# Two transformer blocks in split float32: one weight load for both halves of the activations

## The chip, the cores and the metric

The kernel runs on one core of a Trainium2 chip. The metric is the device time of one launch in microseconds; the time before is the median of three runs. One launch computes both blocks once, for 256 tokens.

## The reference

`reference` sends `x` (256 tokens, 1024 features) through `first_block` and then `second_block`. The first block has two layers, each a mixer and an MLP with a residual around both, and a norm at the end:

```python
for i in range(DEPTH):                 # 2 layers
    hn = rms_norm(x, norm_mix[i])
    mix = even_mixer(...) if i % 2 == 0 else odd_mixer(...)
    x = x + mix
    x = x + sqrelu_mlp(rms_norm(x, norm_mlp[i]), mlp_w1[i], mlp_w2[i])
return rms_norm(x, norm_final)
```

`even_mixer` is a sparse attention beside a differential attention, `odd_mixer` a block attention, each between an input projection and an output projection. `sqrelu_mlp` is `square(relu(hn @ w1)) @ w2` with 4096 hidden features. The second block has one input projection for a convolution with a gated linear recurrence (`xa`, `ga`, 1280 features each), a forgetting attention (`q`, `k`, `v`) and two gates. The branches go through `w_proj_a` and `w_proj_b`, are merged by the gates, and go through `w_out` and a norm; a feed-forward part follows (up to 2 x 3072, convolution, gelu, product, down) with a last norm.

## The kernel before

Activations lie with the features on partitions: `x` is 8 tiles of 128 features by 256 tokens. Nearly all work is products with weights that are read once, as 1 MB chunks (pool `rawp`, 3 buffers, SyncE's queue). A chunk is cut into units of 8 k-tiles by 128 columns, and each unit is split into a high part `whi` (a ScalarE cast, L220) and a low part `wlo` (a VectorE subtraction, L221), both float32r; `w_next` keeps some units ahead. Activations are split in the same way (`split`, L253 to L257): `gh`, `gl` for the normed input of a projection, `hh`, `hl` for the hidden features, `oh`, `ol` for attention outputs, `yh`, `yl` for the recurrence's output. One k-step of a product is three matmuls of 128x128 weights by 256 tokens (`mm3`, L261): high by high, high by low, low by high.

Sums are kept in the PSUM pool `psg`, three buffers of one bank, `[128, 2, 256]`. The order on every engine is that in which the code issues, since the order is fixed by hand: a stage is a generator (`gen_pair`, `gen_nat`, `gen_deep`, `gen_half`), `weave` alternates it with the attention steps, and short work is put off by `later`, `tick` and `pend.step`. `gen_pair` (L384) works on pairs of 128-column tiles, both in one bank, and calls `evac` after the pair. Where a stage begins before its norm is known, it starts on two pairs at once (`kouter`, orders K422, K2, K1). `gen_nat` puts the tokens on the output's partitions, for values. `gen_deep` (L446) is for long sums, one tile per bank (MLP-down, projection a, FFN-down), and `gen_half` (L470) for output projections in two halves of k: the first half is woven with attention and adds to `x`, the second adds, splits and squares for the next norm.

In an MLP, `evac` (L1158) is a VectorE operation that scales by the norm `rb` and clips (L1159), a square (L1160), a cast to `hh` (L253, ScalarE) and the low part `hl` (L254, VectorE). MLP-down adds each tile to `x` (L708) and splits it for the next projection. Output projections add pairs (L718, L726). The norm's factor comes from sums of squares over the features (L317, L324), a diagonal `dg` (L355) and a broadcast product (L360), copied to `rb` (L364). In block 2 projection a multiplies by its gate (L1538), projection b does so and adds (L1550, L1553), and then splits for the projection by `w_out` (o2).

## Time and profile before

| | |
|---|---|
| time, median of three runs | 1174.48 us (1172.11 to 1174.5) |
| span of the profiled execution | 1170.4 us |
| TensorE busy, matmuls | 1138.5 us, 97% |
| TensorE busy, weight loads (beside matmuls) | 1088.1 us, 93% |
| VectorE busy | 793.4 us, 68% |
| ScalarE busy | 625.7 us, 53% |
| GpSimd busy | 190.3 us, 16% |
| DMA | 171 GB/s over the span |

The profiled execution is one of the program; its span runs from the first instruction to the last, and the run's time holds some 4 us more. Matmuls are pipelined, so the duration of one (some 280 ns) says little of its cost; the distance from one start to the next does. A wait is put down to what came last. Stages of the span: layer 0 mixer up to about 155 us, its MLP to 338, layer 1 mixer to 453, its MLP to 638, the recurrence with gates and values to 745, forgetting attention with projections a and b to 910, o2 and its norm to 950, FFN-up to 1065, FFN-down and the last norm to the end.

### The profile page before, as it was taken

How to read it: one execution, taken by the hardware profiler on the slowest of the kernel's cores; microseconds unless marked ns; L12 is line 12 of the kernel's file. 1: busy time of each engine (PE TensorE's matmuls, PEld its weight loads, DVE VectorE, ACT ScalarE, POOL GpSimd, SP SyncE). 2: the span in 40 equal slices, each digit the busy share in tenths (PEclk: the TensorE clock that was granted, in tenths of full speed). 3: DMA queues.
4: the chain of work that ended last, by engine and by line, in shares of the span. 5: the costliest groups of instructions: out<-in, count | busy, mean ns of one | idle time of the engine just before them, and what ended most of it. 6: DMA issues, size and time to landing. Idle time of an engine off the chain costs nothing.

```text
span 1170.4 us, 22694 instructions
## 1 busy us (share of the span) xinstructions
PE 1138.5 (97%) x9343; PEld 1088.1 (93%) x9343; DVE 793.4 (68%) x1404; ACT 625.7 (53%) x1112; POOL 190.3 (16%) x228
## 2 busy tenths in 40 slices
PE   8999999999999999999999999999999999999996
PEld 7987799999999889999999897999999999999996
DVE  5767766674545777566445787766567689999842
ACT  4346555653444545565434577644454556676641
POOL 2014320000010123000001000042310123222211
PEclk9999999999999999999999999999999989999998
DMA  8832244555444334355455453564555525445641
GB/s 331 290 136 73 74 180 145 212 202 199 177 184 180 141 113 145 144 214 206 158 215 198 153 204 109 175 239 141 166 180 197 173 99 167 164 175 180 212 149 36
DMA packets 31303, 200.01 MB, mean 171 GB/s; under 512 B 3594, under 2 KB 6042, under 8 KB 9056
## 3 DMA queue, kind: packets, MB, share of 16 engines
q1 hardware_dynamic: 28832, 187.23, 44.6%
q0 software_dynamic: 2080, 11.08, 2.9%
q8 instruction: 73, 1.20, 0.4%
q14 instruction: 30, 0.25, 0.1%
q10 hardware_dynamic: 288, 0.26, 0.1%
HBM read 197.43 MB, written 3.22 MB: 171 GB/s over the span
## 4 chain that ended last, share of the span: by engine, by line
PE 78%; DVE 14%; ACT 3%; issue 2%; POOL 2%; DMA 1%; SPq 0%; POOLq 0%; ACTq 0%
PE g L262 22%; PE g L264 21%; PE g L263 21%; DVE y L1643 4%; DVE wlo L221 4%; PE rgp L1414 2%; PE g L435 2%; PE g L436 2%; PE g L437 2%; PE pt L623 1%; PE o L673 1%; DVE u L1631 1%; ACT whi L220 1%; PE s L579 1%; DVE y L1655 1%
## 5 line engine op out<-in xcount | busy, mean ns | idle before, releaser
L221 DVE TENSOR_TENSOR wlo<-raw,whi 128x1024 fp32r<-128x1024 f32 (+2 forms) x356 | 420.3, 1212 | 114.2 <-ACT whi L220 113.9
L262 PE MATMUL g<-gh,whi 128*128 128x256 f32 x1632 | 463.7, 284 | 3.2 <-ACT whi L220 1.7
L264 PE MATMUL g<-gh,wlo 128*128 128x256 f32 x1632 | 460.1, 282 | 3.1 <-DVE wlo L221 3.1
L263 PE MATMUL g<-gl,whi 128*128 128x256 f32 x1632 | 457.6, 280 | 0.5 <-DVE gl L257 0.4
L220 ACT CAST whi<-raw 128x1024 fp32r<-128x1024 f32 (+2 forms) x356 | 349.9, 1024 | 18.0 <-PE g L263 8.4
L262 PEld LDWEIGHTS g<-gh,whi 128*128 128x128 f32 x1632 | 309.1, 189 | 10.6 <-issue 5.4
L264 PEld LDWEIGHTS g<-gh,wlo 128*128 128x128 f32 x1632 | 309.2, 189 | 7.2 <-DVE wlo L221 7.1
L263 PEld LDWEIGHTS g<-gl,whi 128*128 128x128 f32 x1632 | 309.4, 190 | 1.1 <-DVE gl L257 0.7
L262 PE MATMUL g<-hh,whi 128*128 128x256 f32 x704 | 199.4, 283 | 1.3 <-DVE u L1631 1.3
L264 PE MATMUL g<-hh,wlo 128*128 128x256 f32 x704 | 199.3, 283 | 0.2 <-DVE wlo L221 0.2
L263 PE MATMUL g<-hl,whi 128*128 128x256 f32 x704 | 199.2, 283 | 0.0
L262 PEld LDWEIGHTS g<-hh,whi 128*128 128x128 f32 x704 | 135.1, 192 | 1.5 <-ACT q L1652 1.5
L264 PEld LDWEIGHTS g<-hh,wlo 128*128 128x128 f32 x704 | 135.1, 192 | 0.4 <-DVE wlo L221 0.4
L263 PEld LDWEIGHTS g<-hl,whi 128*128 128x128 f32 x704 | 135.1, 192 | 0.0
L317 POOL TENSOR_TENSOR acc<-acc,sq 128x256 f32<-128x256 f32 x53 | 42.4, 806 | 465.2 <-ACT sq L313 464.3
L612 POOL TENSOR_TENSOR p<-p,rr 128x384 f32<-128x384 f32 x56 | 50.1, 895 | 205.9 <-DVE rr L607 92.8
L597 ACT ACTIVATE p<-p,nm 128x256 f32<-128x256 f32 x112 | 49.9, 448 | 56.0 <-DVE nm L588 55.8
L1643 DVE SCALAR_TENSOR_TENSOR y<-u,cw,y 128x255 f32<-128x255 f32 (+1 forms) x96 | 60.1, 685 | 0.0
L262 PE MATMUL g<-oh,whi 128*128 128x256 f32 x192 | 55.6, 290 | 0.0
L264 PE MATMUL g<-oh,wlo 128*128 128x256 f32 x192 | 54.3, 283 | 0.0
L263 PE MATMUL g<-ol,whi 128*128 128x256 f32 x192 | 54.2, 282 | 0.0
L1160 ACT ACTIVATE u<-u 128x512 f32<-128x512 f32 x32 | 20.2, 632 | 61.9 <-DVE u L1159 61.9
(317 smaller groups left out, 1455.8 us busy)
## 6 DMA issues: line engine op xcount, KB each, us to landing
raw<-in_w_in_dram SPq DMA_DIRECT2D x30, 1024.0 KB, 4.9
raw<-in_w_up_dram SPq DMA_DIRECT2D x24, 1024.0 KB, 4.9
raw<-in_w_m1a_dram SPq DMA_DIRECT2D x16, 1024.0 KB, 4.8
raw<-in_w_m2a_dram SPq DMA_DIRECT2D x16, 1024.0 KB, 5.0
raw<-in_w_m1b_dram SPq DMA_DIRECT2D x16, 1024.0 KB, 4.9
raw<-in_w_m2b_dram SPq DMA_DIRECT2D x16, 1024.0 KB, 4.9
raw<-in_w_od_dram SPq DMA_DIRECT2D x12, 1024.0 KB, 4.8
raw<-in_w_dn_dram SPq DMA_DIRECT2D x12, 1024.0 KB, 4.8
```

Of the source, the lines that this page charges most:

```text
L220: nc.scalar.copy(out=hi[:, a:b], in_=t[:, off + a:off + b])
L221: nc.vector.tensor_tensor(out=lo[:, a:b], in0=t[:, off + a:off + b], in1=hi[:, a:b].bitcast(F32), op=ALU.subtract)
L262: nc.tensor.matmul(out=o, lhsT=wh, rhs=xh, start=start, stop=False, skip_group_check=skip)
L263: nc.tensor.matmul(out=o, lhsT=wh, rhs=xl, start=False, stop=False, skip_group_check=skip)
L264: nc.tensor.matmul(out=o, lhsT=wl, rhs=xh, start=False, stop=stop, skip_group_check=skip)
L317: nc.gpsimd.tensor_tensor(out=self.acc, in0=self.acc, in1=dst, op=ALU.add)
L435: nc.tensor.matmul(out=ps[:, b, :], lhsT=xh[:, k, bs], rhs=wh[:, k % 4, :], start=(k == 0), stop=False)
L436: nc.tensor.matmul(out=ps[:, b, :], lhsT=xh[:, k, bs], rhs=wl[:, k % 4, :], start=False, stop=False)
L437: nc.tensor.matmul(out=ps[:, b, :], lhsT=xl[:, k, bs], rhs=wh[:, k % 4, :], start=False, stop=(k == KT - 1))
L597: nc.scalar.activation(out=p[:, c0:c1], in_=p[:, c0:c1], func=AF.Exp, scale=-1.0, bias=nm[:, b:b + 1], accum_out=sm[:, b:b + 1],)
L612: nc.gpsimd.tensor_tensor(out=pv, in0=pv, in1=w, op=ALU.mult)
L1643: nc.vector.scalar_tensor_tensor(out=y[:, a, d:], in0=u[:, a, 0:T - d], scalar=cw[:, w, c:c + 1], in1=y[:, a, d:], op0=ALU.mult, op1=ALU.add)
```

## The change

High and low parts of an activation lie side by side in one tile (`Halves`), so that a k-step is two matmuls (`mm2`): the high weights by both parts, 512 columns, into the two halves of a bank, and the low weights by the high part, 256 columns, into the first half. A bank then holds one 128-column tile instead of a pair. The two sums are added afterwards: in `gen_pair` ScalarE copies the second half to the target in SBUF and VectorE adds the first half (`add`, put off by one step); in `take` (projections a and b, FFN-down) the same in one place; for residuals VectorE adds each half to `x` (`add_both`). The values of layer 1 and block 2 use 512-column weights as the moving side (`gen_wide`). The start on two pairs at once, the small gate products, layer 0's values and the last up-projection (block 2's FFN) keep three matmuls. The number of matmul rows of the program goes from 8676 to 6422 on TensorE. Layout changes on the host follow (`_wides`), and some comments are removed. The diff, cut:

```diff
+class Halves:
+
+    def __init__(self, t):
+        self.t = t
+        self.h = t[:, :, 0, :]
+        self.l = t[:, :, 1, :]
+
+    def both(self, k):
+        return self.t[:, k].rearrange("p a t -> p (a t)")
...
-    gh = xp.tile([128, KT, T], FR, name="gh")
-    gl = xp.tile([128, KT, T], FR, name="gl")
+    gg_ = xp.tile([128, KT, 2, T], FR, name="gg_")
+    g_ = Halves(gg_)
+    gh, gl = g_.h, g_.l
...
+    def mm2(ps, wh, wl, X, k, start, stop):
+
+        nc.tensor.matmul(out=ps.rearrange("p a t -> p (a t)"), lhsT=wh, rhs=X.both(k), start=start, stop=False, skip_group_check=True)
+        nc.tensor.matmul(out=ps[:, 0, :], lhsT=wl, rhs=X.h[:, k, :], start=False, stop=stop, skip_group_check=True)
+
+    def take(dst, ps):
+        nc.scalar.copy(out=dst, in_=ps[:, 1, :])
+        nc.vector.tensor_tensor(out=dst, in0=ps[:, 0, :], in1=dst, op=ALU.add)
...
+        wide = getattr(evac, "dst", None)
+        for j in range(j0, npair if wide else 0):
+            D_ = Ctl()
+            for a in range(2):
+                ps = psg.tile([128, 2, T], F32, tag="g", name="g")
+                wh, wl, (nk, ncol) = w_next()
+                if last and j == npair - 1 and a == 1:
+                    w_ahead(4)
+                for k in range(nk):
+                    mm2(ps, wh[:, k, :], wl[:, k, :], X, k, k == 0, k == nk - 1)
+                    if k == 3:
+                        pend.step()
+                        yield
+                if a == 0:
+                    D_.d = wide(first + j)
+                d = D_.d[:, a, :]
+                nc.scalar.copy(out=d, in_=ps[:, 1, :])
+
+                def add(j=j, a=a, d=d, ps=ps, D_=D_):
+                    nc.vector.tensor_tensor(out=d, in0=ps[:, 0, :], in1=d, op=ALU.add)
+                    if a == 1:
+                        pend.ready(lambda: evac(first + j, D_.d))
+
+                later(1, add)
+                pend.step()
+                yield
+        for j in range(npair if wide else j0, npair):
             ps = psg.tile([128, 2, T], F32, tag="g", name="g")
             for a in range(2):
...
-                        mm3(pss_[j][:, 0, :], wh[:, k, :], wl[:, k, :], xh[:, kk, :], xl[:, kk, :], kk == 0, kk == nu * nk - 1)
+                        mm2(pss_[j], wh[:, k, :], wl[:, k, :], X, kk, kk == 0, kk == nu * nk - 1)
...
-                        evac(j, pss_[j][:, 0, :])
+                        evac(j, pss_[j])
...
-            ps = psg.tile([128, 2, T], F32, tag="g", name="g")
             for a in range(2):
+                ps = psg.tile([128, 2, T], F32, tag="g", name="g")
                 for k in range(nk):
-                    mm3(ps[:, a, :], wh[:, k, a * 128:a * 128 + 128], wl[:, k, a * 128:a * 128 + 128],
-                        xh[:, k0 + k, :], xl[:, k0 + k, :], k == 0, k == nk - 1)
-                if a == 0:
-                    tick()
-                    yield
-            evac(j, ps)
-            tick()
-            yield
+                    mm2(ps, wh[:, k, a * 128:a * 128 + 128], wl[:, k, a * 128:a * 128 + 128], X, k0 + k, k == 0, k == nk - 1)
+                evac.wide(j, a, ps)
+                tick()
+                yield
 
...
-            nc.vector.tensor_tensor(out=x[:, j, :], in0=x[:, j, :], in1=ps, op=ALU.add)
+            add_both(j, ps)
...
+    def add_both(i, ps):
+        for s in range(2):
+            nc.vector.tensor_tensor(out=x[:, i, :], in0=x[:, i, :], in1=ps[:, s, :], op=ALU.add)
...
+        def wide(j, a, ps):
+            i = 2 * j + a
+            add_both(i, ps)
+            split(gh[:, i, :], gl[:, i, :], x[:, i, :], V(gain, i))
+            later(2, lambda: norm.add(x[:, i, :]))
+
+        f.wide = wide
...
-        hh = hp.tile([128, 32, T], FR, name="hh")
-        hl = hp.tile([128, 32, T], FR, name="hl")
+        H = Halves(hp.tile([128, 32, 2, T], FR, name="hh"))
+        hh, hl = H.h, H.l
 
         def evac(j, ps):
-            u = hp.tile([128, 2, T], F32, tag="u", name="u", bufs=2)
+            u = ps if j > 1 else evac.dst(j)
...
+        evac.dst = lambda j: hp.tile([128, 2, T], F32, tag="u", name="u", bufs=3)
         pend = Pend(norm)
-        run(gen_pair(16, gh, gl, evac, pend, kouter=K422))
-        run(gen_deep(8, 4, hh, hl, residual_evac(nrm, gain_next, nrm2)))
+        run(gen_pair(16, g_, evac, pend, kouter=K422))
+        run(gen_deep(8, 4, H, residual_evac(nrm, gain_next, nrm2)))
         st.close()
...
-    run(gen_nat(4, gh, gl, evac_v1, pend))
-    run(gen_pair(1, gh, gl, evac_qk("q"), pend))
-    run(gen_pair(1, gh, gl, evac_qk("k"), pend))
+    run(gen_wide(2, gh, gl, evac_v1, pend))
+    run(gen_pair(1, g_, evac_qk("q"), pend))
+    run(gen_pair(1, g_, evac_qk("k"), pend))
...
+        def wide(j, a, ps):
+            i = 2 * j + a
+            t = fp.tile([128, T], F32, tag="pat", name="pbt", bufs=2)
+            take(t, ps)
+            nc.vector.scalar_tensor_tensor(out=t, in0=tb[:, i, :], scalar=1.0, in1=t, op0=ALU.add, op1=ALU.mult)
+            nc.vector.tensor_tensor(out=ta[:, i, :], in0=ta[:, i, :], in1=t, op=ALU.add)
+            if last:
+                split(gh[:, i, :], gl[:, i, :], ta[:, i, :])
...
+    def gen_wide(n, xh, xl, evac, pend):
+
+        for j in range(n):
+            pss_ = [psg.tile([128, 2, T], F32, tag="g", name="g") for _ in range(2)]
+            for u in range(4):
+                wh, wl, (nk, ncol) = w_next()
+                for b in range(2):
+                    bs = slice(b * 128, b * 128 + 128)
+                    o = pss_[b].rearrange("p a t -> p (a t)")
+                    for k in range(2):
+                        kk = 2 * u + k
+                        nc.tensor.matmul(out=o, lhsT=xh[:, kk, bs], rhs=wh[:, k, :], start=(kk == 0), stop=False)
+                        nc.tensor.matmul(out=o, lhsT=xh[:, kk, bs], rhs=wl[:, k, :], start=False, stop=False)
+                        nc.tensor.matmul(out=o, lhsT=xl[:, kk, bs], rhs=wh[:, k, :], start=False, stop=(kk == KT - 1))
+                    if u == 3:
+                        pend.put(lambda j=j, b=b, o=o: evac(j, b, o))
+                    pend.step()
...
-            nc.vector.tensor_tensor(out=mo[:, j, :], in0=mo[:, j, :], in1=nrm.rb, op=ALU.mult)
+            nc.vector.scalar_tensor_tensor(out=mo[:, j, :], in0=mo[:, j, :], scalar=hpost[:, j:j + 1], in1=nrm.rb, op0=ALU.mult, op1=ALU.mult)
...
-        nrm.add(ps)
-        nc.scalar.activation(out=fo[:, j, :], in_=ps, func=AF.Copy, scale=V("fpost2", j))
-
-    run(gen_deep(8, 3, hh, hl, evac_dn, group=3))
+        t = ff.tile([128, T], F32, tag="dnt", name="dnt", bufs=2)
+        take(t, ps)
+        nrm.add(t)

VectorE in MLP-up of layer 0, between the scalings of one pair and of the next. `u` is a pair on its way from PSUM to `hh`, `g` a bank, `wlo` a low weight unit, `gg__91` (below) the tile that holds `gh` and `gl`. Before:

```order
L1159 SCALAR_TENSOR_TENSOR u_2222<-g_2163,rb_2134 128x512
L254 TENSOR_TENSOR hl_1955<-u_2222,hh_1954 128x512
L221 TENSOR_TENSOR wlo_2229<-raw_1871,whi_2228 128x1024
L221 TENSOR_TENSOR wlo_2259<-raw_1964,whi_2258 128x1024
L1159 SCALAR_TENSOR_TENSOR u_2286<-g_2227,rb_2134 128x512
L254 TENSOR_TENSOR hl_1955<-u_2286,hh_1954 128x512
L221 TENSOR_TENSOR wlo_2293<-raw_1964,whi_2292 128x1024
```

After:

```order
L1255 SCALAR_TENSOR_TENSOR u_2121<-u_2121,rb_2019 128x512
L267 TENSOR_TENSOR hh_1851<-u_2121,hh_1851 128x2x256
L234 TENSOR_TENSOR wlo_2153<-raw_1860,whi_2152 128x1024
L451 TENSOR_TENSOR u_2174<-g_2151,u_2174 128x256
L234 TENSOR_TENSOR wlo_2179<-raw_1979,whi_2178 128x1024
L451 TENSOR_TENSOR u_2174<-g_2177,u_2174 128x256
L1255 SCALAR_TENSOR_TENSOR u_2174<-u_2174,rb_2019 128x512
L267 TENSOR_TENSOR hh_1851<-u_2174,hh_1851 128x2x256
```

One add of half a pair now stands behind each weight split, and the scaling (L1255) reads SBUF; scaling and low part still follow each other.

VectorE from the last two pairs of layer 0's output projection to the first scaling of MLP-up. Before, with the residual adds L718, low parts L257, the norm's factor L294 and its diagonal L355:

```order
L718 TENSOR_TENSOR x_90<-x_90,g_1873 128x512
L257 SCALAR_TENSOR_TENSOR gl_92<-x_90,vec_86,gh_91 128x256 x2
L718 TENSOR_TENSOR x_90<-x_90,g_1913 128x512
L257 SCALAR_TENSOR_TENSOR gl_92<-x_90,vec_86,gh_91 128x256 x2
L221 TENSOR_TENSOR wlo_1957<-raw_1666,whi_1956 128x1024
L221 TENSOR_TENSOR wlo_1961<-raw_1666,whi_1960 128x1024
L294 TENSOR_SCALAR rv_2062<-nsum_2058 128x2
L221 TENSOR_TENSOR wlo_2079<-raw_1791,whi_2078 128x1024
L221 TENSOR_TENSOR wlo_2083<-raw_1791,whi_2082 128x1024
L221 TENSOR_TENSOR wlo_2113<-raw_1801,whi_2112 128x1024
L355 TENSOR_SCALAR dg_2128<-cs_87,rn_2061 128x128
L1159 SCALAR_TENSOR_TENSOR u_2136<-g_1966,rb_2134 128x512
```

After, from the third of the last four tiles on:

```order
L789 TENSOR_TENSOR x_90<-x_90,g_1814 128x256 x2
L270 SCALAR_TENSOR_TENSOR gg__91<-x_90,vec_86,gg__91 128x256
L789 TENSOR_TENSOR x_90<-x_90,g_1830 128x256 x2
L270 SCALAR_TENSOR_TENSOR gg__91<-x_90,vec_86,gg__91 128x256
L234 TENSOR_TENSOR wlo_1853<-raw_1576,whi_1852 128x1024
L234 TENSOR_TENSOR wlo_1857<-raw_1576,whi_1856 128x1024
L316 TENSOR_SCALAR rv_1955<-nsum_1951 128x2
L234 TENSOR_TENSOR wlo_1972<-raw_1693,whi_1971 128x1024
L234 TENSOR_TENSOR wlo_1976<-raw_1693,whi_1975 128x1024
L451 TENSOR_TENSOR u_1997<-g_1970,u_1997 128x256
L234 TENSOR_TENSOR wlo_2002<-raw_1703,whi_2001 128x1024
L377 TENSOR_SCALAR dg_2013<-cs_87,rn_1954 128x128
```

Each 128-column tile has its own two adds and its low part, and the add of the first tile of the third pair (L451, `g_1970`) stands ahead of the norm's diagonal (L377).

## Rows read from the trace of the kernel before

**Rows 1.** The page: busy time, and the chain that ended last.

```profile
PE 1138.5 (97%) x9343; PEld 1088.1 (93%) x9343; DVE 793.4 (68%) x1404; ACT 625.7 (53%) x1112; POOL 190.3 (16%) x228
...
PE 78%; DVE 14%; ACT 3%; issue 2%; POOL 2%; DMA 1%; SPq 0%; POOLq 0%; ACTq 0%
```

**Rows 2.** Waits of TensorE over the span: line, releaser, us, times, longest.

```profile
PE pt L623 <- POOL p L612: 5.4, 7, 1.3
PE g L264 <- DVE wlo L221: 3.3, 18, 0.4
```

**Rows 3.** High products of MLP-down, layers 0 and 1: duration ns, first and last start.

```profile
L262 PE MATMUL g<-hh,whi x256: 281/283/283, 245.2 to 337.0; 128*128 128x256 f32 x128
...
L262 PE MATMUL g<-hh,whi x256: 279/283/283, 545.7 to 637.5; 128*128 128x256 f32 x128
```

**Rows 4.** By stage: MLP-up 0, MLP-down 0, MLP-up 1, block 2's xa and ga.

```profile
core 0: us, PE busy (x) PEld busy (x) DVE busy (x) ACT busy (x) POOL busy (x), PEclk, DMA share, GB/s
187.00:245.00 58.00, 58.00 (x514) 58.00 (x514) 40.26 (x45) 34.77 (x45) 0.00 (x0) 1.00 0.58 200
245.00:337.00 92.00, 92.00 (x770) 92.00 (x769) 47.90 (x51) 38.93 (x50) 4.45 (x6) 1.00 0.53 197
480.00:545.00 65.00, 65.00 (x554) 64.97 (x553) 45.33 (x50) 38.30 (x49) 0.00 (x0) 1.00 0.55 195
652.00:715.00 63.00, 63.00 (x482) 52.49 (x481) 56.51 (x103) 45.03 (x77) 0.91 (x4) 1.00 0.42 148
```

**Rows 5.** VectorE in MLP-up of layer 0: start, us, operation [idle before, releaser].

```profile
198.42 1.22 DVE L221 TENSOR_TENSOR wlo<-raw,whi 128x1024 fp32r<-128x1024 f32 x1
199.55 0.68 DVE L1159 SCALAR_TENSOR_TENSOR u<-g,rb 128x512 f32<-128x512 f32 x1
201.59 0.69 DVE L254 TENSOR_TENSOR hl<-u,hh 128x512 fp32r<-128x512 f32 x1 [1.35 <-ACT hh L253]
202.54 2.36 DVE L221 TENSOR_TENSOR wlo<-raw,whi 128x1024 fp32r<-128x1024 f32 x2 [0.26 <-ACT whi L220]
204.83 0.68 DVE L1159 SCALAR_TENSOR_TENSOR u<-g,rb 128x512 f32<-128x512 f32 x1
```

**Rows 6.** One copy from PSUM on ScalarE, one residual add on VectorE: ns.

```profile
L364 ACT COPY rb<-nbc x7: 372/372/373, 28.6 to 957.6; 128x256 f32<-128x256 f32 x7
...
L708 DVE TENSOR_TENSOR x<-x,g x16: 420/422/423, 256.9 to 638.0; 128x256 f32<-128x256 f32 x16
```

**Rows 7.** VectorE in the last half of layer 0's output projection.

```profile
152.49 0.89 DVE L257 SCALAR_TENSOR_TENSOR gl<-x,vec,gh 128x256 fp32r<-128x256 f32 x2 [0.58 <-ACT gh L256]
153.83 2.36 DVE L221 TENSOR_TENSOR wlo<-raw,whi 128x1024 fp32r<-128x1024 f32 x2 [0.45 <-ACT whi L220]
156.11 0.68 DVE L718 TENSOR_TENSOR x<-x,g 128x512 f32<-128x512 f32 x1
```

**Rows 8.** TensorE where that projection ends and MLP-up begins.

```profile
155.33 0.28 PE L264 MATMUL g<-oh,wlo 128*128 128x256 f32 x1
155.44 0.28 PE L262 MATMUL g<-gh,whi 128*128 128x256 f32 x1
```

**Rows 9.** VectorE: norm and first scaling of MLP-up, layer 0, then layer 1.

```profile
170.16 0.28 DVE L355 TENSOR_SCALAR dg<-cs,rn 128x128 f32<-128x128 f32 x1
173.19 0.69 DVE L1159 SCALAR_TENSOR_TENSOR u<-g,rb 128x512 f32<-128x512 f32 x1 [2.74 <-ACT rb L364]
...
471.25 0.69 DVE L1159 SCALAR_TENSOR_TENSOR u<-g,rb 128x512 f32<-128x512 f32 x1 [2.83 <-ACT rb L364]
```

**Rows 10.** VectorE in projection b's last half, and o2's first product on TensorE.

```profile
911.65 0.75 DVE L1550 SCALAR_TENSOR_TENSOR pbt<-tb,g 128x256 f32<-128x256 f32 x2
912.32 0.75 DVE L1553 TENSOR_TENSOR ta<-ta,pbt 128x256 f32<-128x256 f32 x2
913.21 0.76 DVE L1557 TENSOR_TENSOR gl<-ta,gh 128x256 fp32r<-128x256 f32 x2
...
910.58 0.28 PE L262 MATMUL g<-gh,whi 128*128 128x256 f32 x1
```

More of the change, by code (lines that the diff above doesn't have):

```diff
@@ L799 @@
     nlam = ap0.tile([128, 1], F32, name="nlam")
-    wcmp = [ap0.tile([128, 2048], F32, tag="e8", name="wcmp%d" % i, bufs=2) for i in range(2)]
+    wcmps = ap0.tile([128, 2, 2048], F32, tag="e8", name="wcmp")
+    wcmp = [wcmps[:, i] for i in range(2)]
     for i in range(2):
@@ L844, in f, with evac_wide @@
                 nc.scalar.activation(out=d[:, b, c:c + 256], in_=ps[:, b, :], func=AF.Copy, scale=norm.rn[:, b:b + 1])
+        return f
+    def evac_wide(dst):
+        def f(j, b, ps):
+            c = j * 512
+            nc.scalar.activation(out=dst[:, b, c:c + 512], in_=ps, func=AF.Copy, scale=norm.rn[:, b:b + 1])
         return f
@@ L1357, in evac_xa @@
     def evac_xa(j, ps):
-        t = rp.tile([128, 2, 3 + T], F32, tag="xp", name="xp", bufs=2)
-        nc.gpsimd.memset(t[:, :, 0:3], 0.0)
-        nc.vector.tensor_tensor(out=t[:, :, 3:], in0=ps, in1=bc(norm.rb, 2), op=ALU.mult)
+        o = ps if j > 1 else evac_xa.dst(j)
+        t = xps[j]
+        nc.vector.tensor_tensor(out=o, in0=ps, in1=bc(norm.rb, 2), op=ALU.mult)
         def s1():
@@ L1542, in f @@
             t = fp.tile([128, 2, T], F32, tag="qkq", name="pbt", bufs=2)
-            if not last:
-                js = slice(2 * j, 2 * j + 2)
-                nc.vector.scalar_tensor_tensor(out=t, in0=tb[:, js, :], scalar=1.0, in1=ps, op0=ALU.add, op1=ALU.mult)
-                nc.vector.tensor_tensor(out=ta[:, js, :], in0=ta[:, js, :], in1=t, op=ALU.add)
-                return
             for a in range(2):
@@ L1588, in evac_o2 @@
         for a in range(2):
-            i = 2 * j + a
             nrm.add(ps[:, a, :], 0.5)
-        for a in range(2):
-            i = 2 * j + a
-            nc.scalar.activation(out=mo[:, i, :], in_=ps[:, a, :], func=AF.Copy, scale=hpost[:, i:i + 1])
-    run(gen_pair(4, gh, gl, evac_o2, Pend(None), kouter=K422, last=True))
+        if j < 2:
+            for a in range(2):
+                nc.scalar.copy(out=mo[:, 2 * j + a, :], in_=ps[:, a, :])
+    evac_o2.dst = lambda j: mo[:, 2 * j:2 * j + 2, :]
+    run(gen_pair(4, g_, evac_o2, Pend(None), kouter=K422, last=True))
     flush()
@@ L1672, in evac_dn @@
             later(3, nrm.early)
-        nrm.add(ps)
-        nc.scalar.activation(out=fo[:, j, :], in_=ps, func=AF.Copy, scale=V("fpost2", j))
-    run(gen_deep(8, 3, hh, hl, evac_dn, group=3))
+        t = ff.tile([128, T], F32, tag="dnt", name="dnt", bufs=2)
+        take(t, ps)
+        nrm.add(t)
+        nc.scalar.activation(out=fo[:, j, :], in_=t, func=AF.Copy, scale=V("fpost2", j))
+    run(gen_deep(8, 3, H, evac_dn, group=3))
     nrm.part1()
```

140 lines of the change are left out of this document (82 added, 58 removed).

## The prediction

> **What bounds the kernel now.** I read the page first, then TensorE's waits, then the busy time by stage, then single stages on the timeline. The page shows TensorE busy for 1138.5 us of a span of 1170.4 and on 78% of the chain that ended last; VectorE is busy 68% of the time and holds 14% of the chain [rows 1]. TensorE's waits are short: the longest group is 5.4 us and none of the product lines (L262 to L264) waits more than 3.3 us in all [rows 2]. So nearly all time is the matmul stream itself, and the first question is what one matmul costs. In the MLP-down stage of layer 0 the 256 high products start between 245.2 and 337.0 us [rows 3]; with three matmuls each that is 91.8 us over 255 x 3 = 765 starts, 120.0 ns. The stage table gives the other levels: 58 us over 514 matmuls is 113 ns in the up-projection of layer 0, 65 over 554 is 117 ns in that of layer 1 [rows 4]. The granted clock is 1.00 in all of them, the 2.4 GHz level. At one column a cycle (an assumption of mine) 256 columns would take 106.7 ns, so a matmul carries 6 to 13 ns beside its columns.
>
> The second question is what VectorE does in the stages where the change gives it work. In the two MLP up-projections it is nearly full: one pair of tiles costs it 0.68 (scaling by the norm) + 1.35 wait for ScalarE's square and cast + 0.69 (low half) + 0.26 wait + 2.36 (two weight splits), less the overlaps: 204.83 - 199.55 = 5.28 us [rows 5]. TensorE needs 48 x 113 ns = 5.42 us for the same pair, 5.63 in layer 1. There are 0.14 to 0.35 us of room for each pair, and the waits can't be used, since what follows in VectorE's order depends on them.
>
> **Gain: fewer matmuls.** 2032 k-steps change from three matmuls of 256 columns to one of 512 and one of 256, and the value projections of layer 1 and block 2 from 384 matmuls of 256 to 192 of 512. The columns stay the same; a matmul and a weight load go. The trace has no matmul of 512 columns in this type, so its price is bounded. Upper end: twice that of 256 columns, nothing saved (360 ns per step in a 120 ns stage). Lower end: the lowest level, 113, and 106.7 for the second 256 columns, so 113 + 220 = 333, 27 saved. I take the middle: a removed matmul saves what it carried beside its columns, 13.3 ns in the 120 ns stages, 11 in the 117 to 118 ns stages, since the extra is the same for matmuls in one stage and what it hangs on (the instruction or its columns) is open. The Trainium skill, page "TensorE: Matmul & The Clock Gate", section "Back-to-back issue gap", gives N / 2.4 + 2.5 ns for a warm gap, so 109 ns for 256 columns and 216 for 512. This trace disagrees: the 256-column gap is 113 to 120 [rows 3, 4]. By the page a step would be 325 ns.
>
> Only stages that TensorE bounds give this back: MLP-down 512 steps, FFN-down 192, projection a 80, the first halves of three output projections 96: 880 x 13.3 ns = 11.7 us. Layer 0 and layer 1 input projections, gates, q/k of block 2, the rest of o2: 528 x 11 ns = 5.8. Value projections 192 x 11 ns = 2.1. **Sum 19.6 us** (bounds 0 to 37: 880 x 27 + 528 x 20 + 192 x 16 ns, the last from 2 x 118 - 220).
>
> **Loss 1: the two MLP up-projections.** A bank now holds one column tile with its high and low sums, and comes free only after a ScalarE copy (372 ns from PSUM) and a VectorE add of 256 columns (422 ns by itself [rows 6]; right behind another operation it starts 0.08 us before that one's end, as two splits of 1.22 take 2.36 together [rows 5], so it adds 0.34). The copy lies on ScalarE, which waits for TensorE anyway; the two adds per pair go on VectorE's full cycle: 5.28 + 2 x 0.34 to 0.42 = 5.96 to 6.12, taken 6.0. The order shows low half and scaling still side by side, so the 1.35 us wait stays. TensorE then waits for banks, 6.0 a pair instead of 5.42.
>
> The start of the stage is late too. In the last half of layer 0's output projection VectorE has, for a pair, one add of 512 columns (0.68), 0.58 wait and two low halves (0.89) [rows 7]. After the change each tile needs two adds, the wait and a low half: 0.68 + 0.58 + 0.45 = 1.7 us, and four tiles follow the weight splits that end at 156.1. Their adds end at 156.8, 158.5, 160.2, 161.9. The first MLP products need the banks of the second and third of them; they started at 155.44, right after the last projection product [rows 8], and now start at 158.5, 3.1 later. The norm's diagonal (170.16) stands behind the add of the third pair's first tile, and TensorE has half of the next tile, in the same bank, ahead of the broadcast: 0.6 more. So the first scaling, at 173.19, comes at 176.9 [rows 9]. From there: two rounds of 2.65 and an add to the third scaling (182.5), eleven rounds of 6.0 to the fourteenth (248.5), 4.2 to the add that frees the last bank (252.7), 2.7 for the last tile: 255.4. Before, the stage ended at 245.1, just ahead of the first down product [rows 3]. Loss 10.3. In layer 1 the same steps from 471.25 [rows 9] give 553.5 against 545.7 [rows 3], 7.8. **Sum 18.1 us** (16 to 24 by the adds' two prices and 0 to 2 us at the starts).
>
> **Loss 2: other edits.** The last half of projection b: after 911.65 each pair has three double operations, some 2.2 us [rows 10]; after the change each tile has add, scaling, add and low half in a row, 1.4 to 1.6 us. The banks for o2's first products (910.58 before) come free near 913.7 and 915.2: **3.5 us** (2.5 to 5). Block 2's xa and ga stage: VectorE is busy 56.5 of 63 us [rows 4]; 16 adds of 0.34 are 5.4 us, of which TensorE's bank queue covers part: 2 (1 to 6). The tails of o2 and FFN-down: a copy and an add in front of the last squares, 0.8 each. Attention stages: TensorE has other products to issue while a bank is held; 1.5 (0 to 4). The residual adds of the MLP-down stages (two of 422 ns instead of one) have 11.5 us of TensorE time per tile as cover and only the last costs 0.3, in the range. Keys merged into one tile, o2's copies and its scale moved to a later operation: nothing measurable, below 0.5 us either way. The last up-projection, bound by VectorE, keeps three matmuls. **Sum 8.6 us.**
>
> **The forecast.** Losses 26.7, gains 19.6: +7 us on the profiled span, 1170.4 to 1177.4. The span lies 4.1 below the median of three, 1174.5, so 1181.5. The bounds of the known costs alone (gain 10 to 30, losses 21 to 35) give about 1165 to 1200.
>
> **Rivals.**
>
> Rival A, faster: the extra of a matmul is a matter of the instruction, and 512 columns run at the lowest level seen, 333 ns a step. For it: TensorE's stream shows the 113 ns level with the same tiles as the 117 ns level, so columns alone need no more. Against it: two stages never leave 120. The gain is then 37 and the net -10: 1164. By the Trainium skill's gap rule (same page and section) the saving would be an estimated 50 us and the time near 1152; no run here shows it. The point from which A decides is a saving of about 18 ns per k-step, where 1408 steps and the value projections pay the 26.7 us back. Chance 0.28.
>
> Rival B, no difference: VectorE's adds fit into its 1.6 us of waits per pair after all, because with ScalarE's copies the square and cast of a pair find their input earlier; the 6.0 us cycle stays at 5.3, TensorE keeps 5.4, and loss 1 is only the late starts, some 8 us less than summed. The order speaks against it (scaling, then low half, nothing between). 1174. Chance 0.12.
>
> Rival C, the columns cost it all: 512 columns take twice 256 and nothing is saved in the stages bound by TensorE; net +27, 1201. For it: 120 ns could be 0.47 ns a column. With half of the saving it is 1191. Chances 0.08 and 0.12.
>
> **How the numbers follow.** Forecast 0.40, half saving 0.12, none 0.08: slower 0.60. Rival B is "the same" (0.2%, 2.3 us, is about what a measurement of this kernel can tell from no change), 0.12; rival A is faster, 0.28. The range 1161 to 1199 reaches from A's lower side to below C and leaves out C and the tail of A, about 0.15.
>
> **What would show it.** Right: steps of the down stages near 347 ns, so each down tile 11.1 us instead of 11.5; in the up stages VectorE without longer gaps, rounds of 6.0 us, TensorE waiting on the adds of the change; the down stage of layer 0 starting near 255; o2's first product near 3.5 us later relative to the last product of projection b. Wrong: down tiles of 10.7 us or less (rival A) or 11.5 (C); up rounds of 5.4 us (B); TensorE waits in the attention stages of over 4 us, or a granted clock below 1.00 in waits that were not there before, which no term holds.

## The result and the profile after

The change makes the kernel slower: 1221.67 us (median of four runs, 1220.47 to 1224.98) against 1173.93 us, a ratio of 1.041 with a 95% interval of 1.0393 to 1.0428, or 47.7 us by the medians. The forecast had the direction (slower, 0.60) and missed the size: 1181.5, with a range up to 1199. The profile of before is of its run of 1172.11 us and has a span of 1170.4: that run's time holds 1.7 us more than its span, not some 4, and the rest of the 4.1 us up to the median is the spread of the runs.

The page of the profiled execution (span 1223.2 us), busy time and chain, answers to [rows 1]:

```profile
PE 1153.6 (94%) x7119; PEld 985.0 (81%) x7119; DVE 877.4 (72%) x1629; ACT 673.5 (55%) x1266; POOL 187.1 (15%) x228
...
PE 50%; DVE 29%; ACT 11%; issue 5%; DMA 2%; POOL 2%; SPq 0%; POOLq 0%; ACTq 0%
```

TensorE has 2224 matmuls fewer (2032 steps, and 192 of the values) and is busy for longer. Its share of the chain falls from 78% to 50%, VectorE's doubles and ScalarE's goes from 3% to 11%. So the product stream no longer sets the end everywhere. TensorE's waits, by line and releaser (us in total, times, longest), answer to [rows 2]:

```profile
PE pt L695 <- POOL p L684: 8.8, 10, 1.8
PE g L281 <- DVE x L789: 6.1, 2, 3.1
PE g L281 <- DVE pbt L286: 5.1, 4, 3.1
PE g L281 <- DVE u L451: 4.7, 9, 1.0
PE nbc L382 <- DVE dg L377: 4.6, 5, 1.5
...
PE o L745 <- DVE ptsb L701: 2.9, 4, 1.7
PE s L651 <- DVE qkk L1313: 2.3, 4, 1.6
```

The second to fourth lines are waits for banks: the first product of a tile (L281) stands until VectorE has taken the sums out (residual adds L789, `take` L286, adds L451). Before, no product line waited over 3.3 us for one releaser (L262 for three of them 4.5 us; the prediction's "in all" holds for each releaser alone). The last two are attention steps that get their operands later.

What a step costs, in the down stages of both layers (answers to [rows 3]) and on the timeline of a down stage and of block 2's q and k:

```profile
L281 PE MATMUL g<-hh,whi x256: 391/398/403, 269.2 to 359.5; 128*128 128x512 f32 x128
...
L281 PE MATMUL g<-hh,whi x256: 391/398/403, 583.3 to 673.6; 128*128 128x512 f32 x128
...
300.18 0.40 PE L281 MATMUL g<-hh,whi 128*128 128x512 f32 x1
300.42 0.28 PE L282 MATMUL g<-hh,wlo 128*128 128x256 f32 x1
...
799.77 0.39 PE L281 MATMUL g<-gg__91,whi 128*128 128x512 f32 x1
800.00 0.28 PE L282 MATMUL g<-gg__91,wlo 128*128 128x256 f32 x1
800.12 0.40 PE L281 MATMUL g<-gg__91,whi 128*128 128x512 f32 x1
```

90.3 us over 255 steps are 354 ns, against 360 before: 6 ns saved, not 13.3. In block 2 (799.77 to 800.12) a step takes 0.35 us, what three matmuls of 117 to 118 ns took: nothing saved.

VectorE in MLP-up of layer 0 (answers to [rows 5]):

```profile
201.08 0.69 DVE L1255 SCALAR_TENSOR_TENSOR u<-u,rb 128x512 f32<-128x512 f32 x1
203.12 0.69 DVE L267 TENSOR_TENSOR hh<-u,hh 128x512 fp32r<-128x512 f32 x1 [1.35 <-ACT hh L266]
204.07 1.23 DVE L234 TENSOR_TENSOR wlo<-raw,whi 128x1024 fp32r<-128x1024 f32 x1 [0.26 <-ACT whi L233]
205.21 0.42 DVE L451 TENSOR_TENSOR u<-g,u 128x256 f32<-128x256 f32 x1
205.55 1.22 DVE L234 TENSOR_TENSOR wlo<-raw,whi 128x1024 fp32r<-128x1024 f32 x1
206.68 0.42 DVE L451 TENSOR_TENSOR u<-g,u 128x256 f32<-128x256 f32 x1
207.13 0.69 DVE L1255 SCALAR_TENSOR_TENSOR u<-u,rb 128x512 f32<-128x512 f32 x1
```

The round is 207.13 - 201.08 = 6.05 us, the forecast's 6.0, and the 1.35 us wait stays where it was. Where layer 0's output projection ends and MLP-up begins (TensorE, answers to [rows 8]) the reader sees a wait of the forecast length, though ahead of the projection's last tile and not behind it (the first product of MLP-up, at 169.76, follows without a wait), and then something that no term had:

```profile
164.15 0.28 PE L282 MATMUL g<-oht,wlo 128*128 128x256 f32 x1
167.50 0.47 PE L281 MATMUL g<-oht,whi 128*128 128x512 f32 x1 [3.07 <-DVE x L789]
...
168.48 0.63 PE L281 MATMUL g<-oht,whi 128*128 128x512 f32 x1
168.91 0.41 PE L282 MATMUL g<-oht,wlo 128*128 128x256 f32 x1
169.12 0.63 PE L281 MATMUL g<-oht,whi 128*128 128x512 f32 x1
169.55 0.41 PE L282 MATMUL g<-oht,wlo 128*128 128x256 f32 x1
169.76 0.41 PE L275 MATMUL g<-gg__91,whi 128*128 128x256 f32 x1
```

After 3.07 us of idle time matmuls of 512 columns start 430 ns apart from the next and those of 256 some 215. The stage table (the column ahead of the DMA share is the granted clock) gives 0.57 for 168 to 172 us, and the same in layer 1 and at projection b:

```profile
168.00:172.00 4.00, 4.00 (x20) 3.71 (x19) 2.93 (x6) 2.05 (x6) 3.00 (x4) 0.57 0.59 238
482.00:486.00 4.00, 4.00 (x20) 3.71 (x19) 2.90 (x6) 2.14 (x6) 2.99 (x4) 0.57 0.58 238
960.00:964.00 4.00, 4.00 (x18) 3.61 (x19) 2.96 (x8) 1.36 (x4) 0.00 (x0) 0.58 0.75 262
```

The prediction had named two signs against it that no term holds, and both came: this lowered clock, and waits of TensorE of over 4 us in an attention stage. In layer 1's attention (368.7 to 468.2 us) it waits 4.9 us, in the same stretch of before 0.9.

### The profile page after: what moved, and what is told of

Its sections match the earlier page's. It is cut to its first block, busy times and chain, and to the rows that moved or that the text cites. A ratio compares the mean times of both kernels' runs of the same rounds, so it can differ in the third digit from the quotient of the medians.

```text
span 1223.2 us, 18525 instructions
## 1 busy us (share of the span) xinstructions
PE 1153.6 (94%) x7119; PEld 985.0 (81%) x7119; DVE 877.4 (72%) x1629; ACT 673.5 (55%) x1266; POOL 187.1 (15%) x228
## 4 chain that ended last, share of the span: by engine, by line
PE 50%; DVE 29%; ACT 11%; issue 5%; DMA 2%; POOL 2%; SPq 0%; POOLq 0%; ACTq 0%
PE g L281 23%; PE g L282 11%; DVE wlo L234 10%; DVE y L1764 4%; ACT whi L233 4%; PE g L275 2%; PE g L276 2%; PE g L277 2%; DVE u L1255 2%; DMA fb<-scr 2%; DVE u L451 2%; ACT u L1256 2%; ACT hh L266 2%; DVE u L1752 1%; PE pt L695 1%
## 5 line engine op out<-in xcount | busy, mean ns | idle before, releaser
L234 DVE TENSOR_TENSOR wlo<-raw,whi 128x1024 fp32r<-128x1024 f32 (+2 forms) x356 | 424.1, 1211 | 106.4 <-ACT whi L233 105.7
L281 PE MATMUL g<-gg__91,whi 128*128 128x512 f32 x1104 | 401.8, 403 | 8.2 <-DVE u L451 4.7
L233 ACT CAST whi<-raw 128x1024 fp32r<-128x1024 f32 (+2 forms) x356 | 356.2, 1025 | 14.6 <-PE g L276 7.3
L282 PE MATMUL g<-gg__91,wlo 128*128 128x256 f32 x1104 | 311.3, 282 | 0.0
L281 PEld LDWEIGHTS g<-gg__91,whi 128*128 128x128 f32 x1104 | 208.2, 189 | 69.3 <-DVE u L451 15.5
L281 PE MATMUL g<-hh,whi 128*128 128x512 f32 x704 | 249.1, 399 | 1.5 <-DVE u L1752 1.5
L282 PEld LDWEIGHTS g<-gg__91,wlo 128*128 128x128 f32 x1104 | 208.3, 189 | 0.1
L282 PE MATMUL g<-hh,wlo 128*128 128x256 f32 x704 | 198.0, 281 | 0.2 <-DVE wlo L234 0.2
L281 PEld LDWEIGHTS g<-hh,whi 128*128 128x128 f32 x704 | 132.3, 188 | 34.4 <-ACT q L1773 1.8
L277 PE MATMUL g<-gg__91,wlo 128*128 128x256 f32 x528 | 152.7, 289 | 4.0 <-DVE wlo L234 4.0
L275 PE MATMUL g<-gg__91,whi 128*128 128x256 f32 x528 | 151.8, 287 | 4.6 <-ACT whi L233 3.0
L276 PE MATMUL g<-gg__91,whi 128*128 128x256 f32 x528 | 151.1, 286 | 0.5 <-DVE gg__91 L270 0.4
L282 PEld LDWEIGHTS g<-hh,wlo 128*128 128x128 f32 x704 | 133.0, 189 | 1.2 <-DVE wlo L234 1.2
L277 PEld LDWEIGHTS g<-gg__91,wlo 128*128 128x128 f32 x528 | 102.5, 194 | 7.9 <-DVE wlo L234 7.8
L275 PEld LDWEIGHTS g<-gg__91,whi 128*128 128x128 f32 x528 | 102.8, 195 | 6.2 <-ACT whi L233 3.5
L276 PEld LDWEIGHTS g<-gg__91,whi 128*128 128x128 f32 x528 | 102.8, 195 | 1.2 <-DVE gg__91 L270 0.7
L684 POOL TENSOR_TENSOR p<-p,rr 128x384 f32<-128x384 f32 x56 | 49.2, 879 | 221.2 <-ACT p L669 75.5
L789 DVE TENSOR_TENSOR x<-x,g 128x256 f32<-128x256 f32 x80 | 33.5, 418 | 53.6 <-PE g L282 52.2
L1256 ACT ACTIVATE u<-u 128x512 f32<-128x512 f32 x32 | 20.2, 633 | 68.0 <-DVE u L1255 68.0
```

What stands on the lines that cost most here:

```text
L233: nc.scalar.copy(out=hi[:, a:b], in_=t[:, off + a:off + b])
L234: nc.vector.tensor_tensor(out=lo[:, a:b], in0=t[:, off + a:off + b], in1=hi[:, a:b].bitcast(F32), op=ALU.subtract)
L275: nc.tensor.matmul(out=o, lhsT=wh, rhs=xh, start=start, stop=False, skip_group_check=skip)
L276: nc.tensor.matmul(out=o, lhsT=wh, rhs=xl, start=False, stop=False, skip_group_check=skip)
L277: nc.tensor.matmul(out=o, lhsT=wl, rhs=xh, start=False, stop=stop, skip_group_check=skip)
L281: nc.tensor.matmul(out=ps.rearrange("p a t -> p (a t)"), lhsT=wh, rhs=X.both(k), start=start, stop=False, skip_group_check=True)
```

## The experiments

The theory after reading the two traces: 512 columns cost nearly what two times 256 do, so only the long sums gain; everything else pays for taking two sums out of a bank, by VectorE's round in the up-projections, by waits at the output projections with a lowered clock behind them, and by adds in the way of attention. Rivals: the price of 512 columns itself explains the up stages; the waits only move.

The unchanged kernel ran beside each group of runs, with medians from 1173.9 to 1176.5 us, so a difference between two groups is known to some 2 us. "Less" and "more" for edits of the changed kernel are against 1221.67 us.

### The long sums alone

The kernel before, with `mm2` in MLP-down and FFN-down only:

```diff
-  mm3(pss_[j][:, 0, :], wh[:, k, :], wl[:, k, :], xh[:, kk, :], xl[:, kk, :], ...)
+  mm2(pss_[j], wh[:, k, :], wl[:, k, :], X, kk, ...)
```

> The kernel before with only MLP-down and FFN-down on two matmuls per k-step (704 steps), all else as before. Theory 'columns' (a 512-column matmul costs nearly two of 256; in the changed kernel the down step takes 353 ns against 360): 704 x 6.7 ns = 4.7 us less, about 0.8 us given back at the last tiles, so about 1170 us. Theory 'instruction' (a removed matmul gives back what it carries beside its columns, 13.3 ns): 704 x 13.3 = 9.4 less, so about 1165.5 us. If 512 columns cost exactly two of 256: 1174 to 1175.

Measured: 1167.08 us against 1175.18, ratio 0.9935 (0.9923 to 0.9948), 8.1 us. That is near the larger figure. The down stage of layer 0 in its profile:

```profile
L279 PE MATMUL g<-hh,whi x256: 391/394/395, 247.9 to 336.3; 128*128 128x512 f32 x128
```

88.4 us over 255 steps: 347 ns, 13 saved, in layer 1 of the same execution 353. So the forecast's price was within what the long sums show; they do not show one price. This kernel is faster than both others, and the one to keep.

### The MLP up-projections back on three matmuls

```diff
-            u = ps if j > 1 else evac.dst(j)
+            u = hp.tile([128, 2, T], F32, tag="u", name="u", bufs=3)
...
-        evac.dst = lambda j: hp.tile([128, 2, T], F32, tag="u", name="u", bufs=3)
```

> The changed kernel with only the two MLP up-projections back on three matmuls and one bank per pair. Theory 'VectorE': the stage is bound by VectorE's two adds per pair (6.06 us against 5.27), and the add ahead of the norm's diagonal goes as well: 8.0 + 5.6 + about 2 x 1.2 us less, so about 1206 us from 1221.7, and the up stages again 73 and 75.5 us long. Rival 'TensorE': the up stages are longer because a step of 512 + 256 columns costs 353 ns where three of 256 took 340 to 353: then 3 us of the 16 come from that and TensorE shows no waits in the stage either way.

Measured: 1204.01 us (ratio 1.024, 1.0224 to 1.0256), 17.7 less. The up stages are 75.5 and 73.1 us long instead of 81.1. VectorE's theory holds, by size too.

### The output projections back on three matmuls

```diff
+                ps = psg.tile([128, 2, T], F32, tag="g", name="g")
+                for a in range(2):
+                    for k in range(nk):
+                        mm3(ps[:, a, :], wh[:, k, a * 128:a * 128 + 128], wl[:, k, a * 128:a * 128 + 128],
+                            xh[:, k0 + k, :], xl[:, k0 + k, :], k == 0, k == nk - 1)
...
+                evac(j, ps)
```

> The changed kernel with the three output projections (both halves) back on three matmuls and one bank per pair. Theory 'evacuation': their waits for banks (3.1 us each in the last halves, four of 0.5 to 1.3 in projection b's first half) and the lowered clock right behind them go: 5.3 + 3.9 + 9.0 us and 1 to 5 of the attention stages, so 1198 to 1203 us from 1221.7. If the waits only move to the stages behind: less than 9 us.

Measured: 1198.35 us (ratio 1.0204, 1.0188 to 1.0221), 23.3 less, at the upper end of what was expected. None of the stretches behind the output projections has a lowered clock. The waits did not move elsewhere. No run leaves only the adds out here, so adds and banks aren't told apart at the output projections.

### The input projections back on three matmuls

```diff
-  wide = getattr(evac, "dst", None)
+  wide = getattr(evac, "dst", None) if npair == 16 else None
```

> The changed kernel with all input projections, gates, q, k and o2 back on three matmuls (wide values, MLPs, long sums and output projections stay on two). Theory 'in the way': adds and copies on VectorE and ScalarE in the attention and recurrence stages delay the attention steps: 8 to 13 us less, so 1209 to 1214 us from 1221.7. If these stages were lengthened by the output projections' first halves and the clock alone: within 3 us of 1221.7.

Measured: 1208.66 us (ratio 1.0282, 1.0264 to 1.03), 13.0 less. Something is in the way there; what, is asked below.

### All three back

The three edits above together, on the changed kernel.

> The changed kernel with MLP up-projections, output projections and input projections all back on three matmuls; long sums (projection a too) and the wide values stay. If the four parts add up: 1221.7 - 17.7 - 23.3 - 13.0 = 1167.7 us, and what it differs from the run with only the long sums (1167.1) is the price of the wide values and of projection a: 0 to -3 us by saved matmuls.

Measured: 1168.7 us (1168.26 to 1169.63), ratio 0.9934 (0.9919 to 0.9949). The parts add up: 53.0 us instead of 54.0 for their sum. Against the run with only the long sums (1166.43 to 1168.17) wide values and projection a gain nothing: 1.6 us more, of which 1.4 lie between the unchanged kernels beside the two. In the traces projection a takes 38.8 us in both, and the stretch ahead of it, with block 2's values, 185.6 us against 184.4.

### The price by columns

```diff
-                        mm3(pss_[j][:, 0, :], wh[:, k, :], wl[:, k, :], xh[:, kk, :], xl[:, kk, :], kk == 0, kk == nu * nk - 1)
+                        for c in range(2):
+                            cs = slice(c * 128, c * 128 + 128)
+                            mm3(pss_[j][:, 0, cs], wh[:, k, :], wl[:, k, :], xh[:, kk, cs], xl[:, kk, cs], kk == 0 and c == 0, kk == nu * nk - 1, True)
```

> The kernel before, where the long sums (MLP-down, FFN-down, projection a: 784 k-steps) take their products as two matmuls of 128 columns each, six a step in place of three; sums are the same. Theory 'columns' (what a matmul takes beside 106.7 ns goes with its columns): steps stay at 360 ns, time within 3 us of before. Theory 'instruction' (13.3 ns with each matmul): 6 x (53.3 + 13.3) = 400 ns a step, 784 x 40 ns = 31 us more; a down tile 12.8 us instead of 11.5.

Measured: 1415.82 us, 239 more than the unchanged kernel beside it (1176.54). Both theories fall. On the timeline of a down stage:

```profile
299.91 0.28 PE L264 MATMUL g<-hh,wlo 128*128 128x128 f32 x1
300.02 0.28 PE L262 MATMUL g<-hh,whi 128*128 128x128 f32 x1
300.13 0.27 PE L263 MATMUL g<-hl,whi 128*128 128x128 f32 x1
300.25 0.27 PE L264 MATMUL g<-hh,wlo 128*128 128x128 f32 x1
```

A matmul of 128 columns takes 111 ns, nearly as much as one of 256 (113 to 120): below 256 columns, the time of a matmul with its weight load hardly falls with its columns. Whether that is the weight load or a slower rate of the type for few columns wasn't told apart, and so this run can't decide between the theories for 256 columns and more. The spacings in the traces bear on it: 512 columns take 231 to 241 ns, 0.45 to 0.47 ns a column, and 256 take 113 to 120, 0.44 to 0.47 ns a column. So from 256 columns on, what a matmul takes beside one column a cycle goes with its columns. Why it takes more than that is open.

### The lowered clock

```diff
+                if kouter and j == 3 and a == 1:
+                    fps = pst.tile([128, 512], F32, tag="t", name="fps")
+                    for _ in range(25):
+                        nc.tensor.matmul(out=fps[:, 0:256], lhsT=wh[:, 0, 0:128], rhs=xh[:, k0, :], start=True, stop=True)
```

> The changed kernel with 25 matmuls of 256 columns into an unused bank ahead of the last column tile of each output projection's last half, where TensorE waited 3.1 us for a bank; their results are not used. Theory 'clock': the lowered granted clock behind these three waits (170, 484 and 961 us) comes from the waits; with the filling it stays at the 2.4 GHz level there and the last tile and the start of the next stage come back, about 1.7 us at each of three places: about 1216.5 us from 1221.7. If the lowered clock has another cause: not below 1221, later by what the filling overruns.

Measured: 1216.81 us (1215.17 to 1219.61), 4.9 less with 75 more matmuls. The stage table around the wait of layer 0:

```profile
164.00:168.00 4.00, 3.73 (x26) 3.12 (x26) 2.38 (x6) 2.67 (x7) 2.38 (x4) 1.00 0.78 262
168.00:172.00 4.00, 4.00 (x36) 3.97 (x35) 2.50 (x7) 2.13 (x5) 1.71 (x3) 1.00 0.00 0
```

The granted clock stays at 1.00, in the other two places as well. So the lowered clock comes from TensorE's idle time. Its price beside the wait itself is less sure than 4.9 us for three places, since the four runs of either kernel spread by some 4.5 us. In the traces, the stretches from an output projection's first product to the next norm's broadcast are 1.2, 1.1 and 0.9 us shorter than in the changed kernel's second profile (below), 3.1 in all. So it is some 1.0 to 1.6 us a place.

### Adds or copies

```diff
-  later(1, add)
+  add() if npair == 1 else later(1, add)
```

> The changed kernel, where the adds of the single pairs (layer 0's q, k, dq, dk and keys, layer 1's and block 2's q and k) are issued right behind the copy instead of one step later. Theory 'chain': the attention stages wait because copy, put-off add and scaling come one after another before q and k are ready (TensorE's waits for qkk, 2.7 us in all, and the attention steps behind them); issued at once they are ready up to a step earlier and 2 to 5 us come back: 1217 to 1220 us from 1221.7. Theory 'load': what costs is that VectorE and ScalarE do more in these stages; VectorE then stands behind the copy and the time is within 2 us of 1221.7 or longer.

Measured: 1230.51 us (1224.73 to 1232.6), 8.8 more. The theory of the chain falls: TensorE's waits for q and k rise from 2.3 to 6.7 us.

```profile
PE s L651 <- DVE qkk L1313: 6.7, 4, 1.8
```

The time is as the theory of the load has it, but its reason isn't shown: the adds of q and k wait for ScalarE's copies no longer than in the changed kernel (13.3 us in all against 13.7). The time is lost between layer 0's MLP-down and layer 1's output projection (8.9 us longer) and between layer 1's MLP-down and projection a (4.5), with 3.6 back in layer 1's output projection. Why the earlier issue of the adds does this stays open.

The next two leave the add out, for all pairs but the MLP's and for the MLP's alone (the edit, under the condition `npair != 16` or `npair == 16`):

```diff
-  nc.scalar.copy(out=d, in_=ps[:, 1, :])
-  nc.vector.tensor_tensor(out=d, in0=ps[:, 0, :], in1=d, op=ALU.add)
+  nc.scalar.copy(out=d, in_=ps[:, 0, :])
```

> The changed kernel, where the pairs of the input projections, gates, q, k and o2 copy the first half of a bank and leave VectorE's add out (the product with the low activations is missing from these projections): banks, matmuls and ScalarE's copies stay. Theory 'adds': what undoing these projections gave back (13.0 us) is VectorE's adds and the order behind them: 1208 to 1213 us from 1221.7. Theory 'copies and banks': the cost is the copy on ScalarE and one column tile per bank: within 3 us of 1221.7. Between: both.

Measured: 1211.12 us (1208.61 to 1212.48), 10.6 of the 13.0 us. So it is VectorE's adds and the order behind them, with 2.4 us left for copies and banks, hardly more than the 2 us to which such a difference is known.

> The changed kernel, where the MLP up-projections copy the first half of a bank and leave VectorE's add out (the product with the low activations is missing there). Theory 'VectorE': the round goes from 6.06 to 5.3 to 5.4 us, TensorE bounds the stage with 16 x 353 ns = 5.65 us per pair, and each up stage takes 75 to 76 us instead of 81.1; with the add ahead of the norm's diagonal gone 10 to 14 us less: 1208 to 1212. If banks bound the stage, not the adds: up stages of 79 us or more.

Measured: 1204.96 us (1201.0 to 1209.0), 16.7 of the 17.7 us. VectorE's round in the up stage of layer 0:

```profile
205.59 0.68 DVE L1256 SCALAR_TENSOR_TENSOR u<-u,rb 128x512 f32<-128x512 f32 x1
...
210.94 0.68 DVE L1256 SCALAR_TENSOR_TENSOR u<-u,rb 128x512 f32<-128x512 f32 x1
```

5.35 us. With banks and matmuls as in the changed kernel, the up stages take 74.8 us each: in the stage itself the adds are the price, the banks only pass it on. Its late start is another matter. From the norm's sum (L346) to its broadcast (L382) it takes 7.7 us in the changed kernel and 7.7 without the adds, in both layers, and 6.2 in before. With the add gone, there still stands ScalarE's copy, which waits for a tile's products, ahead of a weight cast, its low part on VectorE and the norm's diagonal:

```profile
180.27 0.37 ACT L448 COPY u<-g 128x256 f32<-128x256 f32 x1 [3.52 <-PE g L282]
180.54 1.05 ACT L233 CAST whi<-raw 128x1024 fp32r<-128x1024 f32 x1
...
181.62 1.23 DVE L234 TENSOR_TENSOR wlo<-raw,whi 128x1024 fp32r<-128x1024 f32 x1 [3.17 <-ACT whi L233]
182.76 0.28 DVE L377 TENSOR_SCALAR dg<-cs,rn 128x128 f32<-128x128 f32 x1
```

### Is a stage's level fixed?

```diff
-  for _ in range(9):
+  for _ in range(10):
       nc.tensor.matmul(out=wps[:, 0:128], lhsT=ones, rhs=ones, start=True, stop=True)
```

> The kernel before with ten warming matmuls at the start in place of nine, all else the same. The down and up stages of before take 113, 118 or 120 ns per matmul, each stage its own; with only the long sums changed, the up stages swapped 113 and 118. Theory 'position': the level hangs on where a stage's instructions stand in the program, so one more matmul ahead moves levels in at least one of the four MLP stages and the time by up to 3 us either way. Theory 'tiles' (the level hangs on the tiles' places in SBUF, which do not change): the same levels as before in all four and a time within 1 us.

Measured: 1175.74 us, ratio 0.9997 (0.9988 to 1.0006); layer 0's up stage moved to the 118 ns level (75.5 us).

> The kernel before, unchanged, profiled a second time. Theory 'execution' (the 113 or 118 ns level of a stage changes from one execution to the next): the up stages, 73.1 and 75.5 us long in the first profile, are each one or the other, not all as before. Theory 'position' (fixed by the program): 73.1 and 75.5 us again, 92.0 for both down stages.

Measured: 1176.34 us. The stage table for layer 0's up-projection, unchanged kernel, to be set beside the first line of [rows 4] (514 matmuls in the same 58 us):

```profile
187.00:245.00 58.00, 58.00 (x495) 58.00 (x494) 40.39 (x44) 34.28 (x44) 0.00 (x0) 1.00 0.58 200
```

> The kernel with only the long sums on two matmuls, profiled a second time: its first profile had down stages of 88.6 and 90.3 us and up stages of 75.5 and 73.1 us. Theory 'execution': at least one of the four changes by over 1 us. Theory 'position': the same four lengths within 0.3 us.

Measured: 1167.11 us; down stages 88.6 and 88.7 us, up stages both 75.5. The level of the up stages belongs to the execution, not to the program; the run with one more matmul proves nothing about position. Not all differences are of that kind: the down stages of before took 92.0 us in all three profiles (with one more matmul too), and with two matmuls a step 88.6 to 90.6 us in every run. Why before stands at 120 ns there is open. The profile shown of before was of its fastest run (1172.11), in which that stage had the low level.

> The changed kernel, profiled a second time. If the waits belong to the kernel: up stages of 81.1 us again (VectorE's 6.06 us per pair), last halves of the output projections 5.3, 3.9 and 9.0 us longer than before, lowered clock behind the waits near 170, 484 and 961 us. If the lowered clock were a matter of the single execution: it is missing at one of these places.

Measured: 1220.7 us; up stages 81.1 and 81.0 us, the last halves of layers 0 and 1, from the last attention product on, 3.6 and 3.7 us longer than before, and the whole of projection b 8.6 (in the first profile 5.1, 3.9 and 9.0; it has one more stretch of lowered clock in layer 0, at 150 us), the lowered clock near 166, 480 and 958 us. The waits and what is behind them belong to the kernel.

## Why the prediction was right in direction and wrong in size

Its sum against what the runs gave back when a part was undone (us, losses positive):

| part | forecast | measured |
|---|---|---|
| long sums: MLP-down, FFN-down | -9.4 + 0.8 = -8.6 | -8.1 |
| MLP up-projections, without the output projection ahead | 18.1 - 6.2 = 11.9 | 17.7 |
| output projections, with the late starts | 6.2 + 3.5 - 1.3 = 8.4 | 23.3 |
| input projections, gates, q, k, o2 | 2 + 1.5 + 0.8 - 5.8 = -1.5 | 13.0 |
| wide values, projection a | -2.1 - 1.1 = -3.2 | 1.6, within the spread |
| sum | 7.0 | 47.5 of 47.7 |

The measured column is put together from several kernels: the first row from the long sums added to before, the fifth from the run with all three back against that one, the others from what undoing a part gave back. Its sum tests no more than that the three parts undone add up (54.0 against 53.0 us together).

**What bounds the kernel.** Right: TensorE nearly everywhere, VectorE with little room in the up-projections.

**The price of 512 columns.** Near in size for the long sums, where TensorE has nothing else to wait for: 8.1 us measured in the kernel with these alone, 8.6 forecast. But the saving per step is no fixed price: in the changed kernel's two profiles steps of 354 ns and some of 347 made the three long sums 4.0 and 5.2 us shorter than before, so the hit owes something to the levels of the runs. Wrong to carry it to the other stages: 5.8 + 2.1 + 1.3 + 1.1 us were booked there at 11 to 13 ns a matmul, and none came. The step at fault is "a removed matmul saves what it carried beside its columns" in the 118 ns stages. There a step still takes 350 to 353 ns. Its premise was a cost per matmul; the spacings show a cost per column instead (0.45 to 0.47 ns at 512 columns, 0.44 to 0.47 at 256), so that a removed matmul has next to nothing to give back. Rival C's mechanism ("columns cost it all") held outside the long sums, and 1201 was its price alone; the rest of the miss is in the losses.

**VectorE's round.** Right to 0.05 us: 6.05 against 6.0, and the run without the adds gives back 16.7 of the 17.7 us, by medians of runs that spread by 6 to 8 us. The term was still short by 5.8 us. The traces place some 5.3 us of the miss. The norm's broadcast comes 1.8 to 1.9 us later behind the projection's last product in either layer, where 0.6 was booked; and from the first scaling to the first down product a stage takes 79.9 us, where the sum had 78.5. The prediction laid the 0.6 to the add ahead of the diagonal, but 1.5 us of the delay are there without the add: they come with ScalarE's copy.

**The last halves.** The wait's length was right: 3.1 us forecast for a layer, 6.1 measured for both, and 3.1 at projection b, where 3.5 was booked; its place was off by a tile, since TensorE waits ahead of the last tile and not behind it. Three things were left out. The clock falls behind such a wait: 3.1 to 4.9 us for the three, by the filled kernel. Projection b's first half, booked in no term, is bound by VectorE as well. There each pair takes two adds, two scalings, two adds and a weight split, on VectorE's timeline:

```profile
941.33 1.22 DVE L234 TENSOR_TENSOR wlo<-raw,whi 128x1024 fp32r<-128x1024 f32 x1
942.47 0.42 DVE L286 TENSOR_TENSOR pbt<-g,pbt 128x256 f32<-128x256 f32 x1
942.92 0.43 DVE L1672 SCALAR_TENSOR_TENSOR pbt<-tb,pbt 128x256 f32<-128x256 f32 x1
943.38 0.43 DVE L1673 TENSOR_TENSOR ta<-ta,pbt 128x256 f32<-128x256 f32 x1
943.72 0.42 DVE L286 TENSOR_TENSOR pbt<-g,pbt 128x256 f32<-128x256 f32 x1
944.17 0.42 DVE L1672 SCALAR_TENSOR_TENSOR pbt<-tb,pbt 128x256 f32<-128x256 f32 x1
944.63 0.43 DVE L1673 TENSOR_TENSOR ta<-ta,pbt 128x256 f32<-128x256 f32 x1
944.97 1.22 DVE L234 TENSOR_TENSOR wlo<-raw,whi 128x1024 fp32r<-128x1024 f32 x1
```

3.64 us from split to split, where TensorE needs 8 steps of 353 ns, 2.8; both halves of projection b together take 9.0 us longer than before. And the first halves of layers 0 and 1 delayed the attention woven with them: with three matmuls the stretches from the projection's first product to the last attention product are 3.6 and 1.3 us shorter.

**Attention, recurrence, gates.** Beside the output projections (23.3 against 8.4) the largest miss, 13.0 against -1.5. Of it, 5.8 us are the saving that didn't come; the rest is the step "TensorE has other products to issue while a bank is held; 1.5", with 2 for the recurrence. It asked whether TensorE finds other work, and not who stands behind the add on VectorE. In these stages VectorE serves the attention in order (reductions over rows, copies of transposed blocks, q and k); every add that is put among them, and every add that waits for a copy (13.7 us in all for q and k), comes before a step that TensorE will need. Of the 13.0 us, 10.6 are shown to come with the adds. That they act by this order is read from TensorE's waits in layer 1's attention (4.9 us, 1.5 with three matmuls, 0.9 before) and not tested by itself.

**The rivals.** A (faster) and B (adds hidden in the waits) are excluded by the round of 6.05 us and by the step of 350 ns. C named one of the causes. The range failed because 10.3 us of saving were booked outside the long sums, each loss was bounded by its own wait, and the price of a wait was taken as its length.

## What to carry to other kernels

Before merging matmuls to save instructions, ask what a merged result costs to take out: here two sums per bank cost a copy and an add, the add on the engine that serves everyone in order, and that was nearly seven times the gain (54 us against 8.1). Apply such a change only where a stage is bound by TensorE alone and the extra add has cover, as in the long sums (0.5 to 0.8% faster). Price a new wait of some 3 us on TensorE at its length and a third to a half as much again, since the clock behind it fell here (an estimate from the 3.1 to 4.9 us at three such waits).
